# One pool for the stages of values and joining gate, and a row's running product placed behind the next subtraction, in a hybrid decoder block

## The chip, the cores and the metric

The kernel runs on one core of one Trainium2 chip. The metric is the device time of one execution in microseconds (us); lower is better. Engine names in the profile: PE is TensorE (matmul), PEld its weight loads, DVE is VectorE, ACT is ScalarE, POOL is GpSimd, SP is SyncE, whose queue issues most of the transfers.

## The reference, cut to what matters

One layer of a decoder block over a sequence of 1024 tokens with width 1024, all in float32:

```python
h = rms_norm(x, norm_gain) * (1 + scale) + shift      # scale, shift, gate from c @ w_ada
q, k, v, z_a, u, z_b, m_a, m_b = split(h @ w_in)      # eight blocks of 1024 columns
# attention: 16 heads of 64, strictly causal, stick-breaking
z = q @ k.T / 8
A[t, s] = sigmoid(z[t, s]) * prod_{s < j < t} (1 - sigmoid(z[t, j]))    # s < t
p_a = ((A @ v) * silu(z_a)) @ w_branch_a
p_b = (pool(u) * silu(z_b)) @ w_branch_b              # multi-scale causal pooling
out = x + gate * ((sigmoid(m_a) * p_a + sigmoid(m_b) * p_b) @ w_out)
return rms_norm(out, final_gain)
```

## The kernel before, in words

Every float32 matrix product is made of three matmuls with split operands (high times high, high times low, low times high); the low part is a subtraction `src - high` on VectorE or GpSimd after a copy that rounds to the high part on ScalarE. The tokens are stored in reverse order, so that a row's keys begin at its own block.

The program is a sequence of stages: the norm, the modulation and the pooling projection (to 129 us); the values (names with `vp`, to 205 us); the joining gate m_b (names with `mp`, to 289 us); z_b with the pooled values (`wzb`, to 376 us); the pooling branch (`bp`, to 453 us); the attention with the remaining projections q, k, z_a and m_a (to about 1023 us); the branch of the attention and the output (`pa` and `o`).

**Values, joining gate, pooling branch** all call `seven(nm, sums, load, b_of, a_moves, ta, tb, final, direct)`: a product of 1024 x 1024 matrices in seven products of half size (p1, p5, p6, p7, p4, p3, p2), with sums and differences of the quarter matrices as operands. Each product goes in two halves q of its inner dimension, 24 matmuls each. A left operand starts as one or more raw loads of 512 KB. The first load of it goes to tag `raw` in pool `wts`, which stays open through the whole kernel; the loads that are added to it or subtracted from it (in `a_s1`, for p5, and in `a_s3`, for p7) go to tag `ar` in the pool given as `sums`. `s2k` holds a sum that p5 makes and p6 and p3 use. `a_op` (L546) makes the two parts of the left operand in tag `whl`, `b_op` (L552) those of the right operand in tag `bhl`. `copied` keeps results in tags `s1`, `s2`, `s3`, and `final` gets the finished quarters: `values` (L681) splits them and stores them to `v_d`, `gate_b` (L699) applies the sigmoid and stores them to `sb_d`.

Before the change, the values have a pool `vs` and the gate a pool `ms`, both on the right side of the memory, opened and closed one after the other. `ms` therefore lies where `vs` lay, and its tiles become usable as the tiles of `vs` under them have had their last use. All pools wait by the tile.

**The attention** goes over 8 pairs of heads. A pair has 8 units (p, h, t): a head h and two blocks of 128 queries. `units` in the order of `HT_ORDER` run one step each. In step i:

- `z_items` of the unit 3 places later: for each of its two rows of 128 queries, the logits z in pieces of up to 512 keys on TensorE (bank tag `z`), two sigmoids on ScalarE, `om` for 1 - sigmoid (L921) and `be` for sigmoid (L922), the triangle's mask on GpSimd (L926, twice), then the running product along the row, a scan on VectorE (L928), and the product `be * om` (L929; its line in the profile is that of the helper, L101). Row widths W are 1024 and 896 for t = 0, down to 256 and 128 for t = 3.
- `turn` (L933): a block of the weights `be`, up to four tiles of 128 x 128, is transposed on TensorE into a bank of tag `tr` (two banks; `wt <- ident, be` in the profile), copied on ScalarE (L947, the cast) and subtracted on VectorE (L948). Turned blocks are two ahead of their use (`DEPTH`). `flush()` at the end of `turn` issues what `behind` holds.
- `product`: the turned block times the values (`av`), and at a unit's end `finish`, which adds the parts on VectorE into `tp` (L974), multiplies by `za` on GpSimd (L977) and stores to `ga_d`.
- `fill`: a number of groups of three matmuls of the projections (`p <- hT, w`), spread evenly between the others. Their results go to `use_k`, `use_q`, `use_za` (sigmoid on ScalarE, product on VectorE, L836) or to the gate m_a (`sigmoid_out`, tag `sg`).

The order on each engine: calls wrapped in `order(...)` keep their written order on their engine while `pinned[0]` is set, as it is in the attention, and all matmuls are wrapped. The others (sigmoids, casts, L948, L974, the scan before the change) are placed by the scheduler of the language, which goes by the written order and by when it expects operands to be there; every engine then runs its list strictly in order. Before the change, L929 stands in `behind` with `order`, and the scan is a plain call at the end of its row.

Of the kernel before, what the change touches and what calls it, by code (L numbers as in the profile page):

```python
# [9 lines left out]
F32 = mybir.dt.float32  # L10
# [5 lines left out]
P = 128  # L16
D = 1024
S = 1024
# [33 lines left out]
def block_kernel(ctx, tc, a, out):  # L52
# [3 lines left out]
    def pool(name, **kw):  # L56
        return tc.tile_pool(name=name, bufs=1, reuse_waits="tile", **kw)
# [494 lines left out]
    def b_op(src, pl, bufs, name):  # L552
        hl = pl.tile([P, 2, 2, 512], F32R, tag="bhl", bufs=bufs, name=name)
        act.copy(hl[:, 0], src)
        v.tensor_sub(hl[:, 1], src, hl[:, 0].bitcast(F32))
        return lambda m, e: hl[:, m, e]
# [7 lines left out]

    def seven(nm, sums, load, b_of, a_moves, ta, tb, final, direct):

        s2k = sums.tile([P, 4, 512], F32, name=nm + "s2k")

        def raw(first, m, k, q, name):
            t = (wts if first else sums).tile([P, 2, 512], F32, tag="raw" if first else "ar", bufs=2, name=f"{nm}{name}_{q}")  # L570
            load(t, m, k, q)
            return t

        def a_s1(q):
            r, w = raw(1, 1, 0, q, "a21"), raw(0, 1, 1, q, "a22")
            v.tensor_add(r, r, w)
            w = raw(0, 0, 0, q, "a11s")
            v.tensor_sub(k2(s2k, q), r, w)
            return r

        def a_s3(q):
            r, w = raw(1, 0, 0, q, "a11d"), raw(0, 1, 0, q, "a21d")
            v.tensor_sub(r, r, w)
            return r

        def a_s4(q):
            r = raw(1, 0, 1, q, "a12s")
            v.tensor_sub(r, r, k2(s2k, q))
            return r

        a_of = dict(
            p1=lambda q: raw(1, 0, 0, q, "a11"), p5=a_s1, p6=lambda q: k2(s2k, q), p7=a_s3,
            p4=lambda q: raw(1, 1, 1, q, "a22"), p3=a_s4, p2=lambda q: raw(1, 0, 1, q, "a12"),
        )

        def copied(tag, bufs, j, src):
            t = sums.tile([P, 512], F32, tag=tag, bufs=bufs, name=f"{nm}{tag}_{j}")
            act.copy(t, src)
            return t

        chain, keep = {}, {}
        for name in ("p1", "p5", "p6", "p7", "p4", "p3", "p2"):
            c = {"p5": "b", "p3": "b", "p2": "c"}.get(name, "a")
            if c not in chain:
                chain[c] = [bank((tb if c == "b" else ta)[j // 2], f"{nm}{name}_{j}") for j in range(4)]
            ps = chain[c]
            for q in range(2):
                al, bl = a_op(a_of[name](q), f"{nm}{name}a{q}"), b_of(name, q)
                for j in range(4):
                    js = slice(j * P, j * P + P)  # L610
                    for e in range(2):
                        for i, (w, m) in enumerate(((0, 0), (0, 1), (1, 0))):
                            l, r = (bl(m, e)[:, js], al[:, w, e]) if a_moves else (al[:, w, e, js], bl(m, e))
                            mm(
                                ps[j], l, r, start=name in ("p1", "p5", "p2") and (q, e, i) == (0, 0, 0),
                                stop=(q, e, i) == (1, 1, 2), skip_group_check=True,
                            )
            for j in range(4):
                if name == "p1":
                    keep["s1", j] = copied("s1", 4, j, ps[j])  # L620
                elif name == "p6":
                    keep["s2", j] = copied("s2", 4, j, ps[j])
                elif name == "p7":
                    final(1, 1, j, added(copied("s3", 4, j, ps[j]), chain["b"][j]))
                elif name == "p4":
                    final(1, 0, j, ps[j] if direct else copied("s3", 4, j + 4, ps[j]))
                elif name == "p3":
                    final(0, 1, j, added(keep["s2", j], ps[j]))
                elif name == "p2":
                    final(0, 0, j, added(keep["s1", j], ps[j]))  # L630

    with pool("vp") as vp:

        tq = [vp.tile([P, 4, 512], F32, name=f"ht{i}") for i in range(4)]

        def hq(k, n, q):
            sl = slice(4 * k + 2 * q, 4 * k + 2 * q + 2), slice(512 * n, 512 * n + 512)
            return [t[:, sl[0], sl[1]].bitcast(F32) for t in (h_hi, h_lo)]

        def difference(dst, x, y, name):  # L640
            tmp = vp.tile([P, 2, 512], F32, tag="tmp", bufs=1, name=name)
            v.tensor_sub(dst, x[0], y[0])
            v.tensor_sub(tmp, x[1], y[1])
            v.tensor_add(dst, dst, tmp)

        def without(dst, x, y):
            v.tensor_sub(dst, x[0], y)
            v.tensor_add(dst, dst, x[1])

        def make_t(i, q):  # L650
            dst = k2(tq[i], q)
            if i == 0:
                difference(dst, hq(0, 1, q), hq(0, 0, q), f"tmp0_{q}")
            elif i == 1:
                without(dst, hq(1, 1, q), k2(tq[0], q))
            elif i == 2:
                difference(dst, hq(1, 1, q), hq(0, 1, q), f"tmp2_{q}")
            else:
                without(dst, hq(1, 0, q), k2(tq[1], q))

        for i in reversed(range(KB)):
            ps = any_bank(f"u{i}_1")
            mm3(ps, whl[i], h, range(KB), hmov(1))
            use[i](1, ps)
            make_t((7 - i) // 2, (7 - i) % 2)
        early.close()

        def h_parts(nm, pl):
            def of(name, q):
                if name in ("p1", "p2", "p3"):  # L670
                    k, n = dict(p1=(0, 0), p2=(1, 0), p3=(1, 1))[name]
                    return lambda m, e: hT[:, m, 4 * k + 2 * q + e, 512 * n:512 * n + 512]
                return b_op(k2(tq[("p5", "p6", "p7", "p4").index(name)], q), pl, 2, f"{nm}{name}b{q}")
            return of

        with pool("vs", side="right") as vs:

            def load_v_w(t, m, k, q):
                nc.sync.dma_start(t.rearrange("p k c -> p (k c)"), a["w_v"][m, 2 * k + q])

            def values(m, n, j, src):  # L681
                sb = 4 * n + j
                vo = vs.tile([P, 8, 2, HD], F32R, tag="vo", bufs=3, name=f"vo{sb}_{m}")
                pv = src.rearrange("p (h d) -> p h d", d=HD)
                act.copy(vo[:, :, 0], pv)
                v.tensor_sub(vo[:, :, 1], pv, vo[:, :, 0].bitcast(F32))
                nc.sync.dma_start(
                    v_d[4 * m:4 * m + 4, :, sb].rearrange("n p c -> p n c"),
                    vo.rearrange("p (n h) i d -> p n (h i d)", h=2).bitcast(F32),
                )  # L690

            seven("v", vs, load_v_w, h_parts("v", vs), True, ("av", "tr"), ("pj", "z"), values, True)

        with pool("ms", side="right") as ms:

            def load_m_w(t, m, k, q):
                nc.sync.dma_start(t.rearrange("p k c -> p (k c)"), a["w_mb"][m, 2 * k + q])

            def gate_b(m, n, j, src):  # L699
                t = ms.tile([P, 512], F32, tag="go", bufs=3, name=f"sb{4 * m + j}_{n}")  # L700
                act.activation(t, src, AF.Sigmoid)
                nc.sync.dma_start(sb_d[4 * m + j][:, 512 * n:512 * n + 512], t)

            seven("m", ms, load_m_w, h_parts("m", ms), False, ("pj", "z"), ("av", "tr"), gate_b, True)

    turns[0] = cycle(("av", "tr", "pj", "z"))
    diffs = ExitStack()
# [66 lines left out]
    with pool("at") as at:  # L774
# [63 lines left out]
        def projections():  # L838
# [16 lines left out]
            for i, (ct, p, use) in enumerate(todo):  # L855
# [4 lines left out]
                    load_v(p)  # L860
                gate = use not in (use_k, use_q, use_za)
                if gate:
                    out_ = sigmoid_out(at, 3, use[p], f"m{ct}")
                for sh in range(2):
                    ps = bank("pj", f"p{ct}_{sh}")
                    for kb in range(KB):
# [35 lines left out]
        def z_items(u):  # L902
# [4 lines left out]
            for qb in (2 * t, 2 * t + 1):  # L907
                n0 = qb * P
                W = S - n0
                om = atz.tile([P, S], F32, tag="om", bufs=2, name=f"om{p}_{h}_{qb}")  # L910
                g = t // 2
                be = at.tile([P, S - 512 * g], F32, tag=f"be{g}", bufs=NBE[g], name=f"be{p}_{h}_{qb}")
                nch = (W + 511) // 512
# [1 line left out]
                for i in range(nch):  # L915
# [9 lines left out]
                        for tl, fill in ((om, 1.0), (be, 0.0)):  # L925
                            gp.affine_select(out=tl[:, :P], in_=tl[:, :P], pattern=[[1, P]], compare_op=ALU.is_gt, fill=fill, base=0, channel_multiplier=-1)  # L926
                    if i == nch - 1:
                        v.tensor_tensor_scan(om[:, :W], om[:, :W], om[:, :W], 1.0, ALU.mult, ALU.min)  # L928
                        behind.append(lambda be=be, om=om, W=W: order(v.tensor_mul)(be[:, 1:W], be[:, 1:W], om[:, :W - 1]))  # L929
                        rows.append(be)  # L930
                    yield

# [31 lines left out]
        def finish(u):  # L964
# [2 lines left out]
            del unit_rows[u]  # L967
            av, r = avs.pop(u), half(h)
            if h == 0:
                both[t] = at.tile([P, 256], F32, tag="tp", bufs=3, name=f"tp{p}_{t}")  # L970
            tp = both[t]
            act.copy(tp[r], av[64:128, 0])
            for i in range(2):
# [234 lines left out]
```

## Time and profile before

| what | value |
|---|---|
| median of 3 runs | 1203.88 us (1203.19 to 1203.93) |
| the profiled execution | 1206.08 us, its span 1204.3 us |
| mean granted TensorE clock | 0.996 |
| PE busy | 1174.5 us, 98% |
| PEld busy | 976.4 us, 81% |
| DVE busy | 861.4 us, 72% |
| ACT busy | 563.9 us, 47% |
| POOL busy | 241.6 us, 20% |

The page counts an engine as busy from the start to the end of its instructions; overlapping ones count once. Lines of groups have the line of the kernel, the engine, the operation, what is written and read (names of tiles without their numbers), shapes and count; behind the bar stand the busy time, the mean time of one in ns, and the idle time of the engine just before them with what ended most of it. Lines in order of time begin with start and duration in us; `[0.99 <-DVE wt L948]` says that the engine stood still for 0.99 us before it and what released it. An engine's idle time matters where TensorE ends up waiting for it.

### The profile page before, as it was taken

Reading aid. Unit: us, or ns where it says so; the run is one execution under the profiler, and the core shown is the slowest. Engines: PE = TensorE matmul, PEld = TensorE weight load, DVE = VectorE, ACT = ScalarE, POOL = GpSimd, SP = SyncE. Lnnn points to the kernel's source line nnn. Section 1 sums busy time; section 2 is a strip of 40 time slices with the busy share of each in tenths; the row PEclk is TensorE's granted clock in tenths of the full one; section 3 lists DMA queues with packets and bytes.
Section 4 is the critical chain, followed back from the end, with each engine's and each line's share of the span. In section 5 each row is a group of like instructions: output and inputs, shape, how many; then the busy total and the mean of one; then the engine's idle time right before and its main releaser. Section 6 shows DMA issues by size and latency. Waiting matters only on the chain.

```text
span 1204.3 us, 15853 instructions
## 1 busy us (share of the span) xinstructions
PE 1174.5 (98%) x5602; PEld 976.4 (81%) x5602; DVE 861.4 (72%) x1135; ACT 563.9 (47%) x1042; POOL 241.6 (20%) x376
## 2 busy tenths in 40 slices
PE   8999999899999999999999999999999999999997
PEld 7888888688888887887788878887878888888886
DVE  5767466554997651887888888879788885785643
ACT  5561363363223432656566566665656654232211
POOL 1000000000000003334343443435344441000001
PEclk9999999899999999999999999999999999999999
DMA  9652339546634357232323132422423115975612
GB/s 346 259 186 100 122 106 309 179 137 241 216 106 158 103 176 219 75 93 85 82 71 113 63 104 72 122 71 88 106 83 88 49 66 197 333 267 168 224 65 79
DMA packets 74753, 172.51 MB, mean 143 GB/s; under 512 B 9393, under 2 KB 22833, under 8 KB 72498
## 3 DMA queue, kind: packets, MB, share of 16 engines
q1 hardware_dynamic: 68770, 160.82, 40.9%
q10 hardware_dynamic: 5904, 10.68, 2.5%
q8 instruction: 44, 0.72, 0.2%
q14 instruction: 35, 0.29, 0.1%
HBM read 121.14 MB, written 33.56 MB: 128 GB/s over the span
## 4 chain that ended last, share of the span: by engine, by line
PE 81%; DVE 7%; issue 4%; DMA 4%; ACT 2%; POOL 1%; SPq 0%; POOLq 0%; ACTq 0%; DVEq 0%
PE p L101 21%; PE wzb L101 7%; PE pa L101 7%; PE bp L101 6%; PE o L101 6%; PE vp L101 6%; PE mp L101 5%; PE u L101 5%; PE z L101 4%; PE av L101 4%; PE wt L101 4%; DVE om L928 3%; PE ua L101 3%; PE wm L101 1%; DVE be L101 1%
## 5 line engine op out<-in xcount | busy, mean ns | idle before, releaser
L101 PE MATMUL p<-hT,w 128*128 128x512 f32 x1536 | 392.6, 392 | 0.0
L101 PEld LDWEIGHTS p<-hT,w 128*128 128x128 f32 x1536 | 283.0, 188 | 58.0 <-DVE klo L101 0.3
L928 DVE TENSOR_TENSOR_SCAN om<-om 128x512 f32<-128x512 f32 (+7 forms) x128 | 183.6, 1435 | 52.6 <-POOL om L926 27.4
L116 POOL TENSOR_TENSOR w<-w_raw,w 128x1024 fp32r<-128x1024 f32 x31 | 80.5, 2596 | 458.7 <-ACT w L121 453.6
L921 ACT ACTIVATE om<-z 128x512 f32<-128x512 f32 (+2 forms) x192 | 94.8, 493 | 130.6 <-PE z L101 99.3
L926 POOL TENSOR_SCALAR_AFFINE_SELECT om<-om 128x128 f32<-128x128 f32 x128 | 78.5, 613 | 182.2 <-ACT om L921 162.3
L948 DVE TENSOR_TENSOR wt<-wt,wt 128x512 fp32r<-128x512 f32 (+1 forms) x160 | 99.0, 620 | 20.8 <-ACT wt L947 20.3
L947 ACT CAST wt<-wt 128x512 fp32r<-128x512 f32 (+1 forms) x160 | 88.1, 551 | 46.8 <-PE wt L101 46.0
L101 PE MATMUL av<-wt,vv 128*128 128x512 f32 x320 | 106.0, 412 | 0.3 <-DVE wt L948 0.3
L101 PE MATMUL wt<-ident,be 128*128 128x128 f32 x576 | 90.8, 274 | 13.0 <-DVE wt L948 8.7
L101 DVE TENSOR_TENSOR be<-be,om 128x511 f32<-128x511 f32 (+7 forms) x128 | 101.1, 794 | 1.1
L922 ACT ACTIVATE be<-z 128x512 f32<-128x512 f32 (+2 forms) x192 | 94.1, 490 | 0.0
L101 PEld LDWEIGHTS wt<-ident,be 128*128 128x128 f32 x576 | 68.8, 140 | 30.1 <-DVE wt L948 9.3
L101 PE MATMUL pa<-ga,wa 128*128 128x512 f32 x384 | 89.6, 389 | 0.1
L101 PE MATMUL o<-wo,mhl 128*128 128x512 f32 (+1 forms) x408 | 89.6, 377 | 0.0
L101 PE MATMUL wzb<-hT,wzb 128*128 128x512 f32 x384 | 87.2, 389 | 0.0
L101 PEld LDWEIGHTS o<-wo,mhl 128*128 128x128 f32 x408 | 73.5, 188 | 14.1
L101 PEld LDWEIGHTS pa<-ga,wa 128*128 128x128 f32 x384 | 72.0, 188 | 15.4 <-DVE wa L116 0.5
L101 PEld LDWEIGHTS wzb<-hT,wzb 128*128 128x128 f32 x384 | 72.1, 188 | 15.0
L101 PE MATMUL z<-kl,q 128*128 128x512 f32 (+2 forms) x192 | 65.5, 341 | 0.0
L101 PE MATMUL z<-kh,q 128*128 128x512 f32 (+2 forms) x192 | 64.1, 334 | 1.3 <-DMA q<-qlo 1.3
L101 PE MATMUL u<-hT,wg 128*128 128x512 f32 x240 | 55.5, 391 | 0.0
(261 smaller groups left out, 1692.4 us busy)
## 6 DMA issues: line engine op xcount, KB each, us to landing
w_raw<-in_w_in SPq DMA_DIRECT2D x32, 512.0 KB, 3.5
v_d<-vo SPq DMA_DIRECT2D x16, 512.0 KB, 4.2
vv<-v_d SPq DMA_DIRECT2D x8, 1024.0 KB, 5.3
wa_raw<-in_w_branch_a SPq DMA_DIRECT2D x16, 512.0 KB, 4.6
wa<-in_w_mod SPq DMA_DIRECT2D x7, 1024.0 KB, 7.0
kh<-kh SPq DMA_DIRECT2D x48, 128.0 KB, 2.3
va<-in_w_v SPq DMA_DIRECT2D x10, 512.0 KB, 3.6
ma<-in_w_mb SPq DMA_DIRECT2D x10, 512.0 KB, 4.5
```

What stands on the lines that cost most here:

```text
L101: ins = op(*args, **kw)
L116: lo_eng.tensor_tensor(lo, src, hi.bitcast(F32), op=ALU.subtract)
L921: act.activation(om[:, b0:b0 + n], zp[:, :n], AF.Sigmoid, scale=-0.125)
L922: act.activation(be[:, b0:b0 + n], zp[:, :n], AF.Sigmoid, scale=0.125)
L926: gp.affine_select(out=tl[:, :P], in_=tl[:, :P], pattern=[[1, P]], compare_op=ALU.is_gt, fill=fill, base=0, channel_multiplier=-1)
L928: v.tensor_tensor_scan(om[:, :W], om[:, :W], om[:, :W], 1.0, ALU.mult, ALU.min)
L947: act.copy(wt[:, 0, :off], pt[:, :off])
L948: v.tensor_sub(wt[:, 1, :off], pt[:, :off], wt[:, 0, :off].bitcast(F32))
```

## The change

Two things change. First, the values and the gate take their tiles from one pool `vs`: `s2k` gets a tag of its own with one buffer, `h_parts` no longer takes a pool, `load_v_w` and `load_m_w` become `loads(w)`, and the pool `ms` is gone. The pool is opened on an ExitStack that closes it before `vp`, at the end of the gate stage. Second, in `z_items` the scan moves into `behind`, with `order`, just ahead of the product `be * om`, so that both are issued in `flush()`, behind the subtraction of the next turned block. Tag `om` gets a third buffer, and tags `sg` and `tp` go from three buffers to two.

```diff
-        s2k = sums.tile([P, 4, 512], F32, name=nm + "s2k")
+        s2k = sums.tile([P, 4, 512], F32, tag="s2k", bufs=1, name=nm + "s2k")
...
-    with pool("vp") as vp:
+    with ExitStack() as vps:
+
+        vp = vps.enter_context(pool("vp"))
...
-        def h_parts(nm, pl):
+        vs = vps.enter_context(pool("vs", side="right"))
+
+        def h_parts(nm):
...
-                return b_op(k2(tq[("p5", "p6", "p7", "p4").index(name)], q), pl, 2, f"{nm}{name}b{q}")
+                return b_op(k2(tq[("p5", "p6", "p7", "p4").index(name)], q), vs, 2, f"{nm}{name}b{q}")
...
-        with pool("vs", side="right") as vs:
...
-            seven("v", vs, load_v_w, h_parts("v", vs), True, ("av", "tr"), ("pj", "z"), values, True)
-
-        with pool("ms", side="right") as ms:
...
-            def gate_b(m, n, j, src):
-                t = ms.tile([P, 512], F32, tag="go", bufs=3, name=f"sb{4 * m + j}_{n}")
...
-            seven("m", ms, load_m_w, h_parts("m", ms), False, ("pj", "z"), ("av", "tr"), gate_b, True)
+        def loads(w):
+            def load(t, m, k, q):
+                nc.sync.dma_start(t.rearrange("p k c -> p (k c)"), a[w][m, 2 * k + q])
+            return load
...
+        def gate_b(m, n, j, src):
+            t = vs.tile([P, 512], F32, tag="go", bufs=3, name=f"sb{4 * m + j}_{n}")
...
+        seven("v", vs, loads("w_v"), h_parts("v"), True, ("av", "tr"), ("pj", "z"), values, True)
+        seven("m", vs, loads("w_mb"), h_parts("m"), False, ("pj", "z"), ("av", "tr"), gate_b, True)
...
-                    out_ = sigmoid_out(at, 3, use[p], f"m{ct}")
+                    out_ = sigmoid_out(at, 2, use[p], f"m{ct}")
...
-                om = atz.tile([P, S], F32, tag="om", bufs=2, name=f"om{p}_{h}_{qb}")
+                om = atz.tile([P, S], F32, tag="om", bufs=3, name=f"om{p}_{h}_{qb}")
...
-                        v.tensor_tensor_scan(om[:, :W], om[:, :W], om[:, :W], 1.0, ALU.mult, ALU.min)
-                        behind.append(lambda be=be, om=om, W=W: order(v.tensor_mul)(be[:, 1:W], be[:, 1:W], om[:, :W - 1]))
+
+                        def weights(be=be, om=om, W=W):
+                            order(v.tensor_tensor_scan)(om[:, :W], om[:, :W], om[:, :W], 1.0, ALU.mult, ALU.min)
+                            order(v.tensor_mul)(be[:, 1:W], be[:, 1:W], om[:, :W - 1])
+
+                        behind.append(weights)
...
-                both[t] = at.tile([P, 256], F32, tag="tp", bufs=3, name=f"tp{p}_{t}")
+                both[t] = at.tile([P, 256], F32, tag="tp", bufs=2, name=f"tp{p}_{t}")
```

More of the change, by code (lines that the diff above doesn't have):

```diff
@@ L672, in of @@
                     return lambda m, e: hT[:, m, 4 * k + 2 * q + e, 512 * n:512 * n + 512]
-                return b_op(k2(tq[("p5", "p6", "p7", "p4").index(name)], q), pl, 2, f"{nm}{name}b{q}")
+                return b_op(k2(tq[("p5", "p6", "p7", "p4").index(name)], q), vs, 2, f"{nm}{name}b{q}")
             return of
-        with pool("vs", side="right") as vs:
[L678 to L690, printed above, removed]
-            seven("v", vs, load_v_w, h_parts("v", vs), True, ("av", "tr"), ("pj", "z"), values, True)
@@ L694, in block_kernel @@
-        with pool("ms", side="right") as ms:
-            def load_m_w(t, m, k, q):
-                nc.sync.dma_start(t.rearrange("p k c -> p (k c)"), a["w_mb"][m, 2 * k + q])
-            def gate_b(m, n, j, src):
-                t = ms.tile([P, 512], F32, tag="go", bufs=3, name=f"sb{4 * m + j}_{n}")
-                act.activation(t, src, AF.Sigmoid)
-                nc.sync.dma_start(sb_d[4 * m + j][:, 512 * n:512 * n + 512], t)
-            seven("m", ms, load_m_w, h_parts("m", ms), False, ("pj", "z"), ("av", "tr"), gate_b, True)
+        def loads(w):
+            def load(t, m, k, q):
+                nc.sync.dma_start(t.rearrange("p k c -> p (k c)"), a[w][m, 2 * k + q])
+            return load
@@ new lines, in values @@
+        def values(m, n, j, src):
+            sb = 4 * n + j
+            vo = vs.tile([P, 8, 2, HD], F32R, tag="vo", bufs=3, name=f"vo{sb}_{m}")
+            pv = src.rearrange("p (h d) -> p h d", d=HD)
+            act.copy(vo[:, :, 0], pv)
+            v.tensor_sub(vo[:, :, 1], pv, vo[:, :, 0].bitcast(F32))
+            nc.sync.dma_start(
+                v_d[4 * m:4 * m + 4, :, sb].rearrange("n p c -> p n c"),
+                vo.rearrange("p (n h) i d -> p n (h i d)", h=2).bitcast(F32),
+            )
@@ L706, in block_kernel @@
+        def gate_b(m, n, j, src):
+            t = vs.tile([P, 512], F32, tag="go", bufs=3, name=f"sb{4 * m + j}_{n}")
+            act.activation(t, src, AF.Sigmoid)
+            nc.sync.dma_start(sb_d[4 * m + j][:, 512 * n:512 * n + 512], t)
+        seven("v", vs, loads("w_v"), h_parts("v"), True, ("av", "tr"), ("pj", "z"), values, True)
+        seven("m", vs, loads("w_mb"), h_parts("m"), False, ("pj", "z"), ("av", "tr"), gate_b, True)
     turns[0] = cycle(("av", "tr", "pj", "z"))
```

## The prediction

> **What bounds the kernel now.** I read the page first, then the busy times by stage, then who waited for whom inside the two stages that the diff touches, and at last the instructions in order of time around single stalls.
>
> ```profile
> span 1204.3 us, 15853 instructions
> PE 1174.5 (98%) x5602; PEld 976.4 (81%) x5602; DVE 861.4 (72%) x1135; ACT 563.9 (47%) x1042; POOL 241.6 (20%) x376
> ```
>
> TensorE is busy in 98% of the span, so time is won only where TensorE stands still or runs at a lower clock. The times are of one profiled execution: 1206.08 us, 1.78 us more than its span, and 2.20 us above the median of the runs, 1203.88 us. I work out differences and take them off the median.
>
> The view of busy time by stretch (columns: stretch, length, busy time and count of PE, PEld, DVE, ACT, POOL, then granted clock, DMA share, GB/s):
>
> ```profile
> 129.00:205.20 76.20, 76.20 (x338) 63.10 (x337) 49.34 (x53) 36.35 (x48) 0.00 (x0) 1.00 0.57 190
> 205.20:216.00 10.80, 10.80 (x48) 8.63 (x46) 4.95 (x8) 5.00 (x7) 0.00 (x0) 1.00 0.97 322
> 216.00:220.00 4.00, 0.05 (x2) 0.01 (x1) 3.45 (x3) 2.18 (x4) 0.00 (x0) 0.89 0.18 65
> 220.00:236.00 16.00, 15.25 (x54) 12.05 (x55) 10.02 (x10) 5.04 (x5) 0.00 (x0) 0.81 0.57 194
> 236.00:289.40 53.40, 53.40 (x237) 44.18 (x236) 26.99 (x28) 25.80 (x36) 0.00 (x0) 1.00 0.43 149
> 376.50:453.40 76.90, 76.90 (x337) 63.08 (x337) 49.20 (x48) 34.70 (x42) 2.41 (x1) 1.00 0.47 155
> 500.00:996.00 496.00, 483.00 (x2493) 404.53 (x2492) 419.16 (x563) 304.22 (x660) 203.98 (x300) 1.00 0.29 85
> ```
>
> Rows one, two to five, and six are the three stages of seven products: values, joining gate, and pooling branch. Each has 336 matmuls. The values take 76.2 us and the branch 76.9 us with no gap; the gate takes 10.8 + 4.0 + 16.0 + 53.4 = 84.2 us. It has a hole from 216 to 220 us and then a granted clock of 0.81. The last row is most of the attention: 496 us, of which TensorE stands still for 13.0 us, while VectorE is busy in 419 of 496 us and so has little room.
>
> **The hole in the gate stage.** Groups of matmuls (busy, mean ns | idle before), the chain of work that ended last, and the sync queue:
>
> ```profile
> L101 PE MATMUL vp<-vp5a,vp5b 128*128 128x512 f32 x48 | 11.0, 389 | 0.0
> ...
> L101 PE MATMUL mp<-mp5b,mp5a 128*128 128x512 f32 x48 | 14.0, 460 | 3.9 <-ACT mp5a L548 3.9
> ...
> 209.55 7.99 DMA ma<-in_w_mb
> ...
> 217.64 1.24 DVE ma L576
> ...
> 209.55 1.28 SPq L697 DMA_DIRECT2D ma<-in_w_mb  x1
> ```
>
> The second product (p5) of the gate waits 3.9 us for its left operand. The chain leads back to a load that was issued at 209.55 us, after the values' last tiles, and took 7.99 us; its sum on VectorE began at 217.64 us. That load fills tag `ar` of pool `ms`, which lies where pool `vs` lay. The same product in the values stage waited 0.0 us and took 11.0 us; here it takes 14.0 us, 3.0 us more, at the lower clock.
>
> **Part 1, the shared pool.** No instruction is added or removed. Tags `ar`, `bhl`, `s1` to `s3` and the one `s2k` now serve both stages, and the gate's `ar` slots were last read in the values' fourth product. So the loads of the fifth operand no longer wait for the values' finals. They move ahead on SP's queue, past some of the values' stores, and nothing is queued behind a new wait: the slots are free by then. What remains is the raw half of the operand, in `wts` as before, and the operand slots, which free as the first product's matmuls end, just as in the values stage, where that was hidden. The gain is the length above an undisturbed stage: 84.2 - 76.2 = 8.0 us at most, 84.2 - 76.9 = 7.3 us by the branch. I take 7.7 us, their middle. From below it is bounded by 0: the link of 205 to 216 us has a DMA share of 0.97, and a load that is merely issued earlier could still land late.
>
> **Part 2, the attention.** A row's scan (L928) was issued as soon as its last sigmoid was there, ahead of the next turned block's subtraction (L948); only the product with `be` stood behind that subtraction. Now scan and product both stand behind it, in written order. The same 128 scans run; only their places change. Who waits on TensorE now (total, times, longest), and ScalarE for an `om` buffer:
>
> ```profile
> PE wt L101 <- DVE wt L948: 8.7, 9, 1.8
> PE wt L101 <- POOL tp L977: 2.2, 3, 1.1
> PE wt L101 <- DVE be L101: 1.9, 4, 0.6
> ...
> ACT om L921 <- DVE be L101: 15.4, 9, 2.6
> ```
>
> 8.7 us go to late subtractions (a turn needs the bank that the subtraction two turns ago frees), 1.9 us to late products. The 2.2 us put down to POOL I count with the subtractions, since the waiting instructions are the same turns.
>
> (a) Where the subtraction simply stood behind a scan, its stall goes:
>
> ```profile
> 583.70 3.43 DVE L928 TENSOR_TENSOR_SCAN om<-om 128x640 f32<-128x640 f32 x1 [2.03 <-ACT om L921]
> 587.06 0.66 DVE L948 TENSOR_TENSOR wt<-wt,wt 128x512 fp32r<-128x512 f32 x1
> ...
> 584.81 0.59 ACT L947 CAST wt<-wt 128x512 fp32r<-128x512 f32 x1
> ...
> 587.78 0.66 PE L101 MATMUL wt<-ident,be 128*128 128x128 f32 x4 [1.79 <-DVE wt L948]
> ```
>
> The 3.43 us scan would come after: -1.8 us. This is the one large stall of its kind.
>
> (b) The next pair's first two rows (1024 and 896 wide). Their z work falls into the last steps of a pair, with one turn in a step, so the 1024 scan used to run while the cast of that turn was still being made:
>
> ```profile
> 742.71 2.29 DVE L928 TENSOR_TENSOR_SCAN om<-om 128x1024 f32<-128x1024 f32 x1 [2.20 <-ACT om L921]
> 744.92 0.67 DVE L836 TENSOR_TENSOR za<-p,za 128x512 f32<-128x512 f32 x1
> 745.50 0.68 DVE L948 TENSOR_TENSOR wt<-wt,wt 128x512 fp32r<-128x512 f32 x1
> ...
> 749.81 1.21 DVE L928 TENSOR_TENSOR_SCAN om<-om 128x512 f32<-128x512 f32 x1
> 750.94 0.66 DVE L948 TENSOR_TENSOR wt<-wt,wt 128x512 fp32r<-128x512 f32 x1
> 751.52 1.67 DVE L101 TENSOR_TENSOR be<-be,om 128x895 f32<-128x895 f32 x2
> ...
> 744.82 0.60 ACT L947 CAST wt<-wt 128x512 fp32r<-128x512 f32 x1
> ...
> 752.67 0.49 PE L101 MATMUL wt<-ident,be 128*128 128x128 f32 x3
> ```
>
> From 742.71 to 751.52 us VectorE runs without a gap up to the 895 product, 8.81 us. After the change this run can begin only with the subtraction, whose cast ends at 745.42 us. It loses two pieces: the 512 scan (749.81 to 750.94, 1.13 us), now behind the 895 product, and the `za` product (0.58 us), which fits into the time VectorE now stands idle. The product starts at 745.50 + 8.81 - 1.13 - 0.58 = 752.60 us, 1.08 us later, and ends, with 895/1406 of the 1.67 us, at 753.66 us. The third transposition of the turn at 752.67 us needs it at about 752.9 us: a new stall of some 0.75 us, and 1.1 us where the product was already the last to come. But where the cast was early the same sum turns round:
>
> ```profile
> 546.81 2.36 DVE L928 TENSOR_TENSOR_SCAN om<-om 128x1024 f32<-128x1024 f32 x1 [4.57 <-POOL om L926]
> ...
> 546.91 0.59 ACT L947 CAST wt<-wt 128x512 fp32r<-128x512 f32 x1
> ...
> 555.09 1.67 DVE L101 TENSOR_TENSOR be<-be,om 128x895 f32<-128x895 f32 x2
> ```
>
> 547.50 + (555.09 - 546.81) - 1.13 = 554.65 us, 0.44 us earlier. There are seven such places. Four had a stall (1.9 us in all), 546 among them: 3 x 1.1 + 3 x 0.75 - 0.44 = 5.1 us. That is the dear end; 0 is the cheap one, if every cast is as early as at 546. I take 4.0, nearer to the row that looks like the usual case.
>
> (c) The step after, where the next pair's second rows and four turns meet:
>
> ```profile
> 758.99 2.37 DVE L928 TENSOR_TENSOR_SCAN om<-om 128x1024 f32<-128x1024 f32 x1
> ...
> 768.26 1.22 DVE L928 TENSOR_TENSOR_SCAN om<-om 128x512 f32<-128x512 f32 x1
> 769.39 0.67 DVE L948 TENSOR_TENSOR wt<-wt,wt 128x512 fp32r<-128x512 f32 x1
> ...
> 760.13 0.59 ACT L947 CAST wt<-wt 128x512 fp32r<-128x512 f32 x1
> ...
> 770.12 0.66 PE L101 MATMUL wt<-ident,be 128*128 128x128 f32 x4 [1.05 <-DVE wt L948]
> ```
>
> The run from 758.99 to the subtraction at 769.39 us is 10.40 us. Without the 512 scan and begun at the end of the cast, 760.72 us, the subtraction starts at 760.72 + 10.40 - 1.13 = 769.99 us, 0.6 us later, and the turn at 770.12 us with it. In seven places that is 4.2 us at the dear end. At the cheap end the 2.2 us put down to POOL are gone, since the first subtraction of that step now passes the 896 scan. I take 1.0, the middle.
>
> (d) The third `om` buffer (2 to 3) takes away ScalarE's 15.4 us of waiting, which lies beside TensorE's work; I cost it at nothing, as what it lets start sooner is the scans that now wait for subtractions. If it were missing, the longer life of each `om` would hold up the sigmoids and, behind them on ScalarE, the casts. The buffers given up for it, `sg` and `tp` (3 to 2 each), cost nothing:
>
> ```profile
> ga_d<-tp SPq DMA_DIRECT2D x32, 128.0 KB, 1.8
> sa_d<-m_sg ACTq DMA_DIRECT2D x16, 256.0 KB, 2.0
> ```
>
> A half of a gate takes 24 matmuls, at 76.2/336 = 0.227 us each 5.4 us, against 2.0 us for its store; a `tp` slot is needed again two units later.
>
> **The sum.** -7.7 (pool) - 1.8 (a) + 4.0 (b) + 1.0 (c) = -4.5 us: 1201.6 us for the profiled execution, 1199.4 us for the median.
>
> **The rivals.** Free subtractions: the 8.7 + 2.2 = 10.9 us go entirely and (b) costs 4.4 us, since VectorE idles elsewhere: -7.7 - 6.5, 1189.7 us. For it speaks that every waiting turn names a subtraction or something beside it; against it that VectorE has no gap in the runs of (b) and (c), so it has to do the same work later. Chance 0.22.
>
> Half a hole: the early load lands in the crowded link and half of the 7.7 us stays, 1203.88 - 3.85 + 3.2 = 1203.2 us; against it, the values stage with the same order of loads had no hole. A loss in the attention that just uses up the pool's gain ends in the same place. Chance 0.18. [...]
>
> Late scans, the rival that ends slower: at each of the seven places of (b) the product is 1.1 us later and the `za` product (0.58 us) stays in front of it, 11.8 us; (c) costs its 4.2 us, and (a) gives nothing as another scan is in the way: +16.0 - 7.7, 1212.2 us. It decides from 10.1 us lost in the attention, 0.72 us at each of the fourteen places. For it speaks VectorE's load of 84% in that row; against it the place at 546 us. Chance 0.14.
>
> **How the numbers follow.** The likeliest case has 0.46, with 1195 to 1202.7 us as its own range (attention -1 to +6.5). 0.2%, 2.4 us, is about what a measurement of this kernel can tell from no change. Faster by more: 0.22 and nearly all of 0.46, 0.65. Within: the half hole and the slow edge of the likeliest, 0.21. Slower: 0.14. The range for 8 in 10 goes from 1189.5 us, the free subtractions, to 1206 us, an attention that loses 9.8 us.
>
> **What would show it.** Right: the gate stage at 76 to 77 us with clock 1.00 and no wait before its fifth product; waits of turns for `be` growing from 1.9 to about 6 us; VectorE idle before the 1024 scans, and no subtraction behind one. Wrong: a hole that stays near 216 us, or an attention whose idle time on TensorE leaves 10 to 22 us to either side.

## The result and the profile after

The changed kernel takes 1221.0 us (median of 4 runs, 1219.58 to 1224.66), the kernel before 1203.91 us in runs beside it. The ratio is 1.0145, with an interval of 1.012 to 1.0171. It is slower by 1.45%, above the range of the prediction. One of the six executions of e1, the first experiment below, took 1917.32 us at a granted clock of 0.572, where the five others took 1196.08 to 1201.68 us, and is left out of the median of e1. The profiled execution of the changed kernel took 1222.09 us. Its span and the busy time of the engines, from its page:

```profile
span 1220.4 us, 15852 instructions
PE 1178.8 (97%) x5602; PEld 980.0 (80%) x5602; DVE 871.3 (71%) x1135; ACT 564.8 (46%) x1042; POOL 261.4 (21%) x376
```

The same 5602 matmuls take 4.3 us more than before, though the gate stage lost its slow stretch: somewhere else the clock fell, and its mean over the span is 0.992 in place of 0.996. First the gate stage, by stretch (columns as in the prediction), over the same 84.2 us as before:

```profile
205.20:236.00 30.80, 30.07 (x133) 24.58 (x132) 19.18 (x19) 12.80 (x16) 0.00 (x0) 1.00 0.56 189
236.00:289.40 53.40, 53.40 (x237) 44.23 (x236) 25.25 (x29) 27.15 (x37) 0.00 (x0) 1.00 0.56 187
```

and the group of its second product:

```profile
L101 PE MATMUL mp<-mp5b,mp5a 128*128 128x512 f32 x48 | 11.0, 389 | 0.0
```

The hole and the clock of 0.81 are gone, and the product takes 11.0 us with no wait, as in the values stage. The load that ended the wait before is now issued at 201.72 us in place of 209.55 us, and its sum on VectorE begins at 206.23 us in place of 217.64 us. The next stage begins at 281.81 us in place of 289.27 us: 7.5 us won. From the end of the pooling branch to the start of the attention's branch, however, it takes 593.3 us (445.77 to 1039.06) against 569.8 us (453.24 to 1023.03). The attention lost 23.5 us. Who waits on TensorE in the changed kernel (total, times, longest):

```profile
PE wt L101 <- DVE be L101: 14.4, 7, 2.9
PE wt L101 <- DVE wt L950: 11.0, 11, 3.2
PE wt L101 <- POOL tp L979: 3.4, 3, 2.2
```

and the groups on VectorE (busy, mean ns of one | idle before them, and what ended most of it):

```profile
L101 DVE TENSOR_TENSOR_SCAN om<-om 128x512 f32<-128x512 f32 (+7 forms) x128 | 176.6, 1380 | 2.6 <-POOL om L924 2.5
...
L950 DVE TENSOR_TENSOR wt<-wt,wt 128x512 fp32r<-128x512 f32 (+1 forms) x160 | 99.6, 627 | 75.8 <-ACT wt L949 75.2
...
L101 DVE TENSOR_TENSOR be<-be,om 128x511 f32<-128x511 f32 (+7 forms) x128 | 120.3, 940 | 5.9 <-DVE om L101 0.5
```

Two of these groups in the kernel before:

```profile
L928 DVE TENSOR_TENSOR_SCAN om<-om 128x512 f32<-128x512 f32 (+7 forms) x128 | 183.6, 1435 | 52.6 <-POOL om L926 27.4
...
L948 DVE TENSOR_TENSOR wt<-wt,wt 128x512 fp32r<-128x512 f32 (+1 forms) x160 | 99.0, 620 | 20.8 <-ACT wt L947 20.3
```

Turns wait 14.4 us for products (1.9 us before) and 11.0 us for subtractions (8.7 us before). VectorE's idle time has moved: 2.6 us stand before a scan now (52.6 us before), and 75.2 us before subtractions whose cast isn't there yet (20.3 us before). VectorE takes its list in order, so a scan behind such a subtraction stands still with all its operands ready: at the worst place (below) the row is ready at 807.08 us, VectorE stands idle until 809.89 us, and the scan starts at 810.50 us, behind the subtraction. The products take 120.3 us in all; the kernel that differs only in the place of the scan (e3 below) takes 99.3 us for them.

### The profile page after: what moved, and what is told of

Same layout as the page of the kernel before. It is cut to its first block, busy times and chain, and to the rows that moved or that the text cites. A ratio compares the mean times of both kernels' runs of the same rounds, so it can differ in the third digit from the quotient of the medians.

```text
span 1220.4 us, 15852 instructions
## 1 busy us (share of the span) xinstructions
PE 1178.8 (97%) x5602; PEld 980.0 (80%) x5602; DVE 871.3 (71%) x1135; ACT 564.8 (46%) x1042; POOL 261.4 (21%) x376
## 4 chain that ended last, share of the span: by engine, by line
PE 77%; DVE 11%; issue 5%; DMA 3%; ACT 2%; POOL 1%; SPq 0%; POOLq 0%; DVEq 0%; ACTq 0%
PE p L101 21%; PE wzb L101 7%; PE pa L101 7%; PE o L101 6%; PE bp L101 6%; PE vp L101 6%; PE u L101 4%; PE mp L101 4%; PE z L101 4%; DVE om L101 4%; PE av L101 4%; PE wt L101 4%; PE ua L101 3%; DVE be L101 2%; DVE wt L950 2%
## 5 line engine op out<-in xcount | busy, mean ns | idle before, releaser
L101 PE MATMUL p<-hT,w 128*128 128x512 f32 x1536 | 397.8, 396 | 1.0 <-DVE klo L101 1.0
L101 PEld LDWEIGHTS p<-hT,w 128*128 128x128 f32 x1536 | 286.8, 190 | 60.6 <-DVE klo L101 1.5
L101 DVE TENSOR_TENSOR_SCAN om<-om 128x512 f32<-128x512 f32 (+7 forms) x128 | 176.6, 1380 | 2.6 <-POOL om L924 2.5
L950 DVE TENSOR_TENSOR wt<-wt,wt 128x512 fp32r<-128x512 f32 (+1 forms) x160 | 99.6, 627 | 75.8 <-ACT wt L949 75.2
L924 POOL TENSOR_SCALAR_AFFINE_SELECT om<-om 128x128 f32<-128x128 f32 x128 | 92.6, 724 | 182.8 <-ACT om L919 143.5
L101 DVE TENSOR_TENSOR be<-be,om 128x511 f32<-128x511 f32 (+7 forms) x128 | 120.3, 940 | 5.9 <-DVE om L101 0.5
L101 PE MATMUL wt<-ident,be 128*128 128x128 f32 x576 | 92.5, 277 | 29.1 <-DVE be L101 14.4
```

Of the source, the lines that this page charges most:

```text
L101: ins = op(*args, **kw)
L950: v.tensor_sub(wt[:, 1, :off], pt[:, :off], wt[:, 0, :off].bitcast(F32))
```

## The experiments

Several chips were used. Each ratio is to runs of the kernel before on the same chip; 0.01 of it is 12 us.

**Which part.** e1 makes the change to the pool alone: the scan goes back in front, and the buffers are as before.

```diff
-                        def weights(be=be, om=om, W=W):
-                            order(v.tensor_tensor_scan)(om[:, :W], om[:, :W], om[:, :W], 1.0, ALU.mult, ALU.min)
...
+                        v.tensor_tensor_scan(om[:, :W], om[:, :W], om[:, :W], 1.0, ALU.mult, ALU.min)
+                        behind.append(lambda be=be, om=om, W=W: order(v.tensor_mul)(be[:, 1:W], be[:, 1:W], om[:, :W - 1]))
```

> Only the shared pool; scan and the buffers of om, sg and tp as before the change. The trace after the change has the gate stage at some 77 us against 84.2 us before. If the loss comes from the attention part alone, this gives 1203.9 - 7.6 = 1196.3 us, with the hole before the gate's fifth product gone and the attention as before (waits of turns on TensorE about 12.8 us). If sharing the pool also moves something in the attention (its start, the memory under it), it gives more than 1200 us.

Measured: 1197.76 us, ratio 0.9938 (0.9917 to 0.9959). The pool alone wins, and the turns' waits for subtractions (8.0 us) and products (1.9 us) are close to those of before; only what is put down to `tp` is longer (5.2 us against 2.2 us).

e2 is the opposite, the part in the attention on the two old pools:

```diff
-        vs = vps.enter_context(pool("vs", side="right"))
+        with pool("vs", side="right") as vs:
...
+        with pool("ms", side="right") as ms:
```

> Only the attention part (scan behind the subtraction, three om buffers, two sg and two tp), on the two separate pools of before. If the two parts add up: 1221.0 + 7.6 = 1228.6 us, with the hole of 3.9 us back. If they work on each other, it lands elsewhere: below 1224 us the pool has a share in the loss.

Measured: 1228.63 us, ratio 1.0189 (1.0167 to 1.0211). 1.0189 x 0.9938 is 1.0126, within the interval of the whole change: the two parts account for it, and a third effect, if there is one, is lost in the width of these intervals (about 0.2% each way, 2.5 us). The loss is the attention's.

e3 keeps everything of the change, the three buffers included, and puts only the scan back in front:

```diff
-                            order(v.tensor_tensor_scan)(om[:, :W], om[:, :W], om[:, :W], 1.0, ALU.mult, ALU.min)
+                        v.tensor_tensor_scan(om[:, :W], om[:, :W], om[:, :W], 1.0, ALU.mult, ALU.min)
```

> The changed kernel with the scan put back in place ahead of the subtraction; shared pool, three om buffers and two sg and tp buffers kept. Theory 'place of the scan': the whole loss goes, 1194 to 1197 us, and VectorE's idle time lies ahead of the scans again (about 50 us) and not ahead of the subtractions. Rival 'buffers': the two buffers given up, or the third om buffer, cost in the attention, and this stays above 1210 us.

Measured: 1197.94 us, ratio 0.9931 (0.9908 to 0.9955), as e1. The buffers neither cost nor win anything that these runs can tell. Its waits on TensorE:

```profile
PE wt L101 <- DVE wt L946: 8.7, 9, 1.8
PE wt L101 <- POOL tp L975: 2.3, 3, 1.1
...
PE wt L101 <- DVE be L101: 1.3, 3, 0.6
...
PE wt L101 <- POOL om L924: 0.6, 1, 0.6
```

So the place of the scan costs 1.0145 - 0.9931, some 26 us, or 25.3 us between the two spans (1220.4 and 1195.1). It is made up of the turns' waits, 28.8 us after (the sum of the three rows of after) against 12.9 us here, +15.9, and TensorE's busy time, 1178.8 against 1170.3 us for the same matmuls, +8.5: together 24.4 of the 25.3 us.

**Which rows.** e4 leaves the scans of the two widest rows in front and puts the narrower ones behind:

```diff
-                            order(v.tensor_mul)(be[:, 1:W], be[:, 1:W], om[:, :W - 1])
...
+                        wide = W >= 896
+                        if wide:
+                            v.tensor_tensor_scan(om[:, :W], om[:, :W], om[:, :W], 1.0, ALU.mult, ALU.min)
+                        else:
+                            behind.append(scan)
+                        behind.append(lambda be=be, om=om, W=W: order(v.tensor_mul)(be[:, 1:W], be[:, 1:W], om[:, :W - 1]))
```

> The changed kernel with the scans of the rows 1024 and 896 wide in place, and the six narrower rows' scans behind the subtraction as changed. Theory 'late start of the wide rows': nearly all of the loss goes, 1193 to 1199 us, and the waits of turns for be fall from 14.4 us to under 3 us. Rival 'every deferred scan costs': only a third goes (the wide rows are 32 of 128 scans), so more than 1210 us.

Measured: 1190.21 us, ratio 0.9874 (0.985 to 0.9899), faster than both kernels and 3 us below the range that was expected. Its waits on TensorE:

```profile
PE wt L101 <- POOL tp L982: 4.8, 4, 1.7
...
PE wt L101 <- DVE wt L953: 0.9, 2, 0.7
PE wt L101 <- DVE be L101: 0.5, 1, 0.5
```

With the wide scans in front, the idea of the change is right for narrow rows. Their scans behind the subtraction take the waits for subtractions from 8.7 to 0.9 us, and 7.7 us off the time (e3 to e4, same chip). The wide rows lose 1.0145 - 0.9874 = 0.0271, some 33 us (30.8 us between the medians).

e5 turns the condition round, e10 keeps only the 1024 row in front:

```diff
-                        wide = W >= 896
+                        wide = W < 896      # e5
+                        wide = W == 1024    # e10
```

> The mirror of the run with the wide rows in place: only the scans of the rows 1024 and 896 wide stand behind the subtraction, the narrower rows' scans are in place; shared pool and the three om buffers as changed. If the two kinds of rows add up: all in place was 1197.9 us, narrow behind 1190.2 us (-7.7), all behind 1221.0 us, so wide alone behind gives 1221.0 + 7.7 = 1228.7 us. If the loss comes from narrow scans that pile up behind the wide ones, it stays below 1215 us.

Measured: 1248.71 us, ratio 1.0358 (1.0335 to 1.0381). This missed by 20 us. The turns wait 42.2 us in all (18.8 for products, 15.9 for subtractions, 4.0 for a mask on GpSimd, 3.5 for `tp`), and TensorE is busy for 1186.0 us. With wide rows behind, narrow scans in front are worse than behind, the reverse of what they are with wide rows in front. So the effects of the two kinds of rows don't add; what makes the 20 us wasn't followed up.

> The changed kernel with only the scans 1024 wide in place; 896 and narrower behind. Theory 'late start of the pair's first row' (the scan 1024 wide used to fill the time in which the cast was made): most of the 30.8 us between all behind and both wide in place comes back, 1190 to 1200 us. Rival 'both wide rows cost alike': about half, 1203 to 1208 us.

Measured: 1203.82 us, ratio 0.9994 (0.9983 to 1.0005). The theory that only the first row's late start matters falls, and the rival's range holds: with the 1024 rows in front, 896 rows behind still cost 0.9994 - 0.9874, 14 us.

**Which unit.** The wide rows come twice in each pair, in the unit of head 0, part (b) of the prediction, and that of head 1, part (c). e14 and e15 put one of the two back in front:

```diff
-                        wide = W >= 896
+                        wide = t == 0 and h == 0    # e14
+                        wide = t == 0 and h == 1    # e15
```

> The changed kernel; only the two wide scans of a pair's first unit (h, t) = (0, 0) in place, those of (1, 0) and all narrower ones behind the subtraction. Theory: the waits for be (14.4 us) all belong to the first unit, whose rows are turned one step after their z, and the clock's fall after stalls over 2 us hangs mostly on them; so some 17 of the 30.8 us between all behind (1221.0) and both units in place (1190.2) come back: 1200 to 1206 us, with waits for be under 2 us. Rival, both units alike: 1205.6 us, with the waits for be halved.

> The mirror: only the wide scans of unit (1, 0) in place, those of (0, 0) behind. Theory: the waits for be stay near 14 us and the waits for subtractions go: 1206 to 1212 us. Rival: the two units' losses hang together (one delay feeds the next), then this one comes back below 1200 us or not at all.

Measured: e14 1204.6 us, ratio 0.9987 (0.9974 to 1.0); e15 1207.2 us, ratio 1.0012 (0.9998 to 1.0027). The waits on TensorE in e14, with head 1 behind:

```profile
PE wt L101 <- DVE wt L953: 10.9, 11, 3.2
PE wt L101 <- POOL tp L982: 3.5, 3, 2.2
PE wt L101 <- DVE be L101: 0.5, 1, 0.5
```

and in e15, with head 0 behind:

```profile
PE wt L101 <- DVE be L101: 14.4, 7, 2.9
PE wt L101 <- POOL tp L982: 4.7, 4, 1.8
...
PE wt L101 <- DVE wt L953: 0.9, 2, 0.7
```

The times alone don't decide between the theory of e14 and its rival, which gave 1205.6 us; the waits do. Head 0 behind makes nearly all the waits for products (14.4 us, against 0.5 us in e14), head 1 behind nearly all those for subtractions (10.9 us, against 0.9 us in e15). Against e12 (below; both wide rows in front, same chip, 1190.34 us; its buffers differ, but e4 with the buffers of e14 and e15 has the same ratio within the intervals) head 1 behind costs 14.3 us and head 0 behind 16.9 us, together 31.1 us, which is the loss of the wide rows. So the two losses add, and the rival of e15 falls. In these profiles TensorE is busy 5.9 us longer in e14 than in e12 (1175.5 and 1169.6 us) and 1.8 us longer in e15 (1171.4 us), at mean clocks of 0.995 in e14, 0.998 in e15 and 0.999 in e12: the part of the loss that comes from a lower clock is larger with head 1 behind, not with head 0 as was expected.

**Late start or collisions with GpSimd.** Some of the wide products take more than twice their time when GpSimd subtracts for a weight split beside them (a 1023 product of the changed kernel 3.05 us in place of 1.21 us). e6 and e7 take that subtraction away: ScalarE writes a copy in its place. e6 has the scan in front, e7 behind.

```diff
-        lo_eng.tensor_tensor(lo, src, hi.bitcast(F32), op=ALU.subtract)
+        if lo_eng is gp:
+            act.copy(lo, src)
+        else:
+            lo_eng.tensor_tensor(lo, src, hi.bitcast(F32), op=ALU.subtract)
```

> The scan in place, shared pool and three om buffers, and GpSimd's split of the projections' weights taken away: the low part is a copy on ScalarE in its stead, so the subtraction of the high part is left out (the low part is wrong). It is the base for the next run: 1185 to 1198 us, without stretched scans of 3.4 us and more.

> The changed kernel, scan behind, with GpSimd's split of the weights taken away in the same way (the subtraction of the high part is left out). Theory 'late start': the distance to the run with the scan in place and no split stays at 15 to 23 us, as with the split (1221.0 - 1197.9 = 23.1 us). Rival 'collisions' (products on VectorE that take 2.2 to 3.4 us in place of 1.1 to 1.2 us beside GpSimd's split): the distance falls below 8 us.

Measured: e6 1194.34 us, ratio 0.9917 (0.9902 to 0.9932); e7 1210.67 us, ratio 1.0051 (1.0036 to 1.0066). The waits of e7:

```profile
PE wt L101 <- DVE be L101: 12.9, 8, 3.2
PE wt L101 <- DVE wt L953: 8.7, 8, 2.6
```

Without any such collision (the products take 97.7 us in all, and the 1023 products 1.22 us in the mean, against 1.54 us in the changed kernel) the distance between front and behind is 16.3 us, of some 23 to 26 us with them. So the late start, less what the narrow rows win, is worth about 16 us by itself, and the rest, 7 to 10 us, comes with GpSimd's subtractions. Much of that rest seems to be the clock: in the profiled executions TensorE's busy time grows by 1.3 us from e6 to e7 (1171.0 to 1172.3), and by 8.5 us from e3 to the changed kernel; the mean clock goes from 0.999 to 0.997 and from 0.999 to 0.992. ScalarE's extra copies load both kernels alike (591.3 us busy in e6 and 592.2 us in e7), but VectorE's subtractions wait 89.0 us for casts in e7, against 75.2 us in the changed kernel, so the split is rough.

**Better versions.** e12 is e4 with the old buffers (two for `om`, three for `sg` and `tp`); e13 is e4 with the 768 rows in front too:

```diff
-                        wide = W >= 896
+                        wide = W >= 768     # e13
...
-                om = atz.tile([P, S], F32, tag="om", bufs=3, name=f"om{p}_{h}_{qb}")
+                om = atz.tile([P, S], F32, tag="om", bufs=2, name=f"om{p}_{h}_{qb}")    # e12
```

> Wide scans in place, narrow ones behind, with the buffers of before: two om, three sg, three tp. If the third om buffer has a part in the 1190.2 us, since a deferred row holds its buffer longer, this is slower by 3 us or more. If not, it stays within 2 us of it.

> As the run with the wide scans in place, with the 768 wide ones in place too: only 640 and narrower stand behind. The products with be of width 767 took 1260 ns there against 952 ns before, which speaks for 1187 to 1190 us; if the gain of 7.7 us came from the 768 rows, the first to meet a waiting subtraction, it goes up to 1193 to 1198 us.

Measured: e12 1190.34 us, ratio 0.9867 (0.985 to 0.9884): the third `om` buffer has no effect here either. e13 1188.81 us, ratio 0.9857 (0.9838 to 0.9875), the fastest, though its interval overlaps that of e4. Both beat the kernel before and the change.

## Why the prediction was wrong

**The pool: right.** -7.7 us forecast, -7.5 us measured in the trace; the stage, its clock, the earlier load and the absent wait are as it said.

**(a) Scans in front of subtractions: right in kind, too small.** It counted one stall of 1.8 us. The narrow rows behind win 7.7 us (e3 to e4), nearly all of the 8.7 us of waits for subtractions. The other eight of those waits, 6.9 us in all, go too when the narrow scans stand behind, and the step left them out.

**(b) The unit of head 0: the step that failed most.** +4.0 us forecast, 16.9 us measured (e15 against e12); 13.9 us of it are waits for products. The mechanism, a run of work that begins later, was right, even at the place that was worked out. VectorE at that place after the change:

```profile
742.81 0.69 DVE L950 TENSOR_TENSOR wt<-wt,wt 128x512 fp32r<-128x512 f32 x1 [0.76 <-ACT wt L949]
743.42 2.28 DVE L101 TENSOR_TENSOR_SCAN om<-om 128x1024 f32<-128x1024 f32 x1
...
745.93 1.21 DVE L101 TENSOR_TENSOR be<-be,om 128x1023 f32<-128x1023 f32 x1
...
747.40 0.67 DVE L950 TENSOR_TENSOR wt<-wt,wt 128x512 fp32r<-128x512 f32 x1
747.99 2.01 DVE L101 TENSOR_TENSOR_SCAN om<-om 128x896 f32<-128x896 f32 x1
749.92 0.53 DVE L950 TENSOR_TENSOR wt<-wt,wt 128x384 fp32r<-128x384 f32 x1
750.37 1.07 DVE L101 TENSOR_TENSOR be<-be,om 128x895 f32<-128x895 f32 x1
```

The 895 product was to start 8.81 - 1.13 - 0.58 = 7.10 us after the first subtraction; it starts after 750.37 - 742.81 = 7.56 us. The 0.46 us are another subtraction, at 749.92, which the scheduler put between scan and product and which no term of the sum had. TensorE at this place and at the worst of the seven:

```profile
751.50 0.33 PE L101 MATMUL wt<-ident,be 128*128 128x128 f32 x1 [1.10 <-DVE be L101]
...
820.42 0.33 PE L101 MATMUL wt<-ident,be 128*128 128x128 f32 x1 [2.88 <-DVE be L101]
```

1.10 us where 0.75 us was forecast. But this place is the mildest of the seven; the stalls there are 1.69, 2.72, 1.91, 1.10, 2.88, 1.66 and 2.42 us, their mean 2.05 us. In all they grew by 12.5 us (from 1.9 to 14.4 us), not by 4.0. One place was worked out and taken for the usual one, and the one counted with a gain of 0.44 us, at 546 us before, has a stall of 1.69 us after in place of 0.59 us:

```profile
539.86 0.69 DVE L950 TENSOR_TENSOR wt<-wt,wt 128x512 fp32r<-128x512 f32 x1 [5.29 <-ACT wt L949]
...
546.98 0.66 DVE L834 TENSOR_TENSOR za<-p,za 128x512 f32<-128x512 f32 x1
547.56 0.54 DVE L950 TENSOR_TENSOR wt<-wt,wt 128x384 fp32r<-128x384 f32 x1
548.02 1.07 DVE L101 TENSOR_TENSOR be<-be,om 128x895 f32<-128x895 f32 x1
```

By the sum the product starts 555.09 - 546.81 - 1.13 = 7.15 us after the first subtraction; it starts after 8.16 us, and the 1.01 us are about the `za` product (0.58 us) and the subtraction (0.46 us) in front of it. Such a subtraction stands there at six of the seven places. And at the three places with the longest stalls (2.72, 2.88 and 2.42 us) an instruction of the run, beside GpSimd's subtraction, took 1.2 to 1.8 us more than elsewhere. So the sum lacked two terms: what the scheduler puts into VectorE's list ahead of the product, and what GpSimd adds to it. The worst place, on VectorE,

```profile
809.89 0.69 DVE L950 TENSOR_TENSOR wt<-wt,wt 128x512 fp32r<-128x512 f32 x1 [4.91 <-ACT wt L949]
810.50 2.28 DVE L101 TENSOR_TENSOR_SCAN om<-om 128x1024 f32<-128x1024 f32 x1
...
813.01 3.05 DVE L101 TENSOR_TENSOR be<-be,om 128x1023 f32<-128x1023 f32 x1
...
818.85 0.52 DVE L950 TENSOR_TENSOR wt<-wt,wt 128x384 fp32r<-128x384 f32 x1
819.29 1.07 DVE L101 TENSOR_TENSOR be<-be,om 128x895 f32<-128x895 f32 x1
```

on ScalarE, where the row's last piece of `om` is written,

```profile
806.48 0.60 ACT L919 ACTIVATE om<-z 128x512 f32<-128x512 f32 x1
...
809.27 0.59 ACT L949 CAST wt<-wt 128x512 fp32r<-128x512 f32 x1
```

and on GpSimd:

```profile
811.89 3.08 POOL L116 TENSOR_TENSOR w<-w_raw,w 128x1024 fp32r<-128x1024 f32 x1 [2.15 <-ACT w L121]
```

The row is ready at 807.08 us, VectorE is idle for 4.91 us, and yet the scan starts only at 810.50 us, 3.4 us late, because the cast ahead of it ends at 809.86 us. Then the 1023 product, 1.21 us elsewhere, takes 3.05 us while GpSimd subtracts. The same place with the scan in front (e3):

```profile
797.74 2.29 DVE L926 TENSOR_TENSOR_SCAN om<-om 128x1024 f32<-128x1024 f32 x1 [2.54 <-ACT om L919]
...
802.87 3.87 DVE L926 TENSOR_TENSOR_SCAN om<-om 128x896 f32<-128x896 f32 x1 [0.26 <-ACT om L919]
...
807.57 1.07 DVE L101 TENSOR_TENSOR be<-be,om 128x895 f32<-128x895 f32 x1
```

Here too an instruction takes longer beside GpSimd's subtraction (the 896 scan 3.87 us, not 2.0), and from the start of the first scan to the end of the 895 product it takes 10.90 us, against 9.86 us after the change. The run of work isn't longer after the change; it begins later, and that makes the stall: counted from the end of the row's last piece of `om`, the 895 product ends after 11.00 us in e3 and after 13.28 us here, 2.28 us later, and the stall behind it grows from 0.50 to 2.88 us.

**(c) The step after, the unit of head 1: mis-sized.** +1.0 us forecast, 4.2 us at its dear end, 14.3 us measured (e14 against e12). The waits in e14 show the mechanism it named, a subtraction behind a late run, but 10.9 us of it in place of 0.9 us, and TensorE is busy 5.9 us longer, which no term had. The cheap end, a first subtraction that passes the 896 scan, did not come: e14's 3.5 us put down to `tp` against 4.8 us in e4 are a gain of 1.3 us only.

**What no step had: the clock.** The prediction put a price only on the stalls; before the change, 500 to 996 us of the attention, with stalls of up to 1.8 us, showed a clock of 1.00. After the change TensorE is busy 8.5 us longer than in e3. Four microseconds from the end of the stall at 820.42 us, by stretch (clock third from the end):

```profile
820.40:824.40 4.00, 3.98 (x13) 3.18 (x14) 3.83 (x6) 1.44 (x3) 0.00 (x0) 0.67 0.00 0
```

In 820.40 to 824.40 us 13 matmuls run where 18 run at full clock (e15, below). Five of the nine stalls above 1.6 us, all of 2.18 us and more, were followed by 0.57 to 0.67 over such a stretch; the four of up to 2.00 us were not. At these clocks (0.61, 0.67, 0.57, 0.58 and 0.64) the five stretches lack 4 x 1.93 = 7.7 us of full clock, nearly all of the 8.5 us.

**(d) Buffers: right.** Nothing, by e3 and by e12.

**The rivals.** The late scans came, with a chance of 0.14, and their price of +16.0 us in the attention was still too small, against 23.5 us, though they gave (a) nothing, where the narrow rows win 7.7 us. The argument against them, the place at 546 us, was one place, and it was misread: its product came later, not earlier. The argument for them, VectorE's load of 84%, may have been the better one; that a late run of 9 us can't be caught up where little idle time follows was not tested by itself.

**The sum with the measured terms.** -7.5 (pool) - 7.7 (a) + 16.9 (b) + 14.3 (c) = +16.0 us, against 17.1 us between the medians of the changed kernel and the kernel before.

## What to carry to other kernels

An instruction that is moved behind another on an in-order engine waits for all that the other waits for. Compare, at every place and not at one, when the mover's operands are ready and when the new predecessor's are; here, with the long scans in front, short ones won by the edit by which the long ones lost, so try the move by size. And price a new stall on TensorE with the clock that may follow it, not by its length alone: here five of the nine stalls above 1.6 us were followed by 0.57 to 0.67, by the sum above 7.7 us in all.

## What the runs showed of the hardware

**The clock fell after some stalls of about 2 us and more, not after each.** Stalls on TensorE in three of the kernels, and the four microseconds from their end. In e15:

```profile
816.43 0.33 PE L101 MATMUL wt<-ident,be 128*128 128x128 f32 x1 [2.88 <-DVE be L101]
```

```profile
816.43:820.43 4.00, 4.00 (x18) 3.33 (x19) 3.83 (x6) 2.03 (x5) 0.00 (x0) 1.00 0.00 0
```

In e14:

```profile
893.07 0.44 PE L101 MATMUL wt<-ident,be 128*128 128x128 f32 x2 [1.96 <-DVE wt L953]
```

```profile
893.07:897.07 4.00, 4.00 (x15) 3.39 (x16) 4.00 (x7) 0.96 (x2) 0.00 (x0) 0.65 0.46 98
```

In e7:

```profile
682.53 0.33 PE L101 MATMUL wt<-ident,be 128*128 128x128 f32 x1 [3.20 <-DVE be L101]
```

```profile
682.50:686.50 4.00, 3.97 (x18) 3.33 (x19) 3.83 (x6) 1.43 (x4) 0.00 (x0) 1.00 0.00 0
```

The stall of 2.88 us, the same as that of after at 820.42 us, kept the full clock here and not there; 3.20 us kept it, and 1.96 us did not. So the length alone doesn't decide; what does, no run here shows.

**VectorE beside a GpSimd subtraction.** Where a subtraction of 128x1024 on GpSimd ran beside them, a 1023 product took 3.05 us (1.21 us elsewhere) and an 896 scan 3.87 us (2.0 us). In e7, without these subtractions, the sixteen 1023 products took 1.22 us in the mean (1.54 us in the changed kernel) and the sixteen 896 scans 2.03 us (2.10 us in the changed kernel). In both cases it looks like waiting rather than sharing, though no run shows what the instruction would wait for: the product ends at 816.06 us, 1.09 us after GpSimd's subtraction (814.97 us), and the scan at 806.74 us, 1.88 us after it (804.86 us), each a little less than the instruction takes alone. GpSimd's subtraction took 3.08 us beside the product and 2.40 us beside the scan; the median of the 31 in the changed kernel is 2.41 us.
